# Turned tiles through SyncE's queue, weight transfers queued apart from their split, and consumers one unit later, in a two-layer encoder trunk

## The chip, the cores and the metric

The kernel runs on one core of one Trainium2 chip. The metric is device microseconds of one execution, the median of the runs; less is better. The profile is one further execution, taken by the hardware profiler.

## The reference, cut to what matters

Input is `x` of 256 rows by 2048, in float32. Layer 1 is forgetting attention with an MLP, layer 2 is chunked attention against a shared K/V with another MLP:

```python
u = rms_norm(h, a_norm_g)
q, k, v, fz = jnp.split(u @ a_w_in, [D, 2 * D, 3 * D], axis=-1)      # D = 2048, 16 heads of 128
q = rms_norm(q per head, a_q_g);  k = rms_norm(k per head, a_k_g)
s = q @ k.T * scale + c[query] - c[key]      # c: running sum of log sigmoid(fz + b_f), causal
h = h + (softmax(s) @ v) @ a_w_out
h = h + relu(rms_norm(h) @ w1)**2 @ w2       # w1: 2048 x 8192, w2: 8192 x 2048
k_sh, v_sh = jnp.split(rms_norm(h) @ kv_w, [D], axis=-1);  k_sh = rms_norm(k_sh per head)
q = rms_norm(rms_norm(h) @ b_w_q per head)
s = q @ k_sh.T * scale + rel_bias            # causal in chunks of 64
h = h + (softmax(s) @ v_sh) @ b_w_out
h = h + relu(rms_norm(h) @ w1)**2 @ w2       # second layer's weights
```

All products with weights are of float32 accuracy. The weights come to about 400 MB and each is read once.

## The kernel before, in words

**Units and panels.** Weights are cut into 768 units of 128 partitions by 1024 float32 (512 KB). A unit is loaded into a `raw` tile by SyncE's queue (SP, line 114; four `raw` buffers), and split on the chip into `hi` (ScalarE, line 116, rounded to float32r) and `lo` (VectorE, line 117, the rest), three buffers each. A panel is 8 units: 256 rows by 512 columns of output, accumulated in PSUM. For each unit the function `products` (lines 294 to 296) makes 12 matmuls of 128x512: hi·hi, hi·lo and lo·hi for two k-tiles and two row blocks. `fetch` keeps the splits of two units ahead of the one that is multiplied (`AHEAD = 2`); `issue` queues a unit's transfer and its split together. 8 units make a panel, and the units run in this order: layer 1's q, k and v panels for each of four head groups (units 0 to 95), its output projection (96 to 127), its MLP in four chunks of w1 and w2 (128 to 383), layer 2's q (384 to 415), the shared k and v by head group (416 to 479), output projection (480 to 511), MLP (512 to 767). Where a stage is `woven`, its first two panels alternate unit by unit.

**Turning a tile.** What comes out of a panel has its rows on partitions; the next product needs columns there. `blocks32` (line 168) transposes 32x32 blocks on VectorE into a tile `z`. `carry` moves the blocks through DRAM: `rows` (line 178) writes `z` to the DRAM tile `turn` in one DMA, `columns` (line 184) reads it back in four DMAs of 32 partitions. Both are issued by GpSimd (POOL), `nc.gpsimd.dma_start`. There are 92 such round trips: 60 of 512 KB (hidden activations, q, k and residual panels) and 32 of 192 KB (one for each head's softmax, through `flip`).

**The list of fills.** `run_fill` runs once behind each unit's products and takes the next entry of the deque `fill`; `add_fill` lays a list of entries over it. `carry` returns `[[rows], [], [columns]]`: rows behind the first unit after the panel, columns behind the third. The consumers lie further back: the hidden activations' `take` (lines 513 to 519), the residual panels' `use` (`split_turned`, lines 160 to 162) and `scale_q` (line 337) behind the sixth unit; in `attend`, the four heads' `softmax` (lines 352 to 369) behind units 6 to 9 of the v panel and what follows, and `values` (lines 382 to 386) behind units 13 to 16.

**What sets the order.** Each engine executes its own list of instructions in order, and waits on semaphores. These lists are not the order in which the Python code names the operations: the framework places each engine's instructions by a plan of its own when the program is built, with the code's order as a priority. So the place of a fill in the code is a wish, and the profile shows the place that was given.

Of the kernel before, what the change touches and what calls it, by code (L numbers as in the profile page):

```python
# [10 lines left out]
F32R = mybir.dt.float32r  # L11
# [4 lines left out]
P = 128  # L16
# [10 lines left out]
NEG = -1.0e30  # L27
UN = 1024
AHEAD = 2
UA = UN // 512  # L30
REL = 384

# [2 lines left out]
def trunk(ctx: ExitStack, tc: tile.TileContext, xT, xr, gs, hg, bf, wgate, w_in, w_oa, w1a, w2a,  # L35
          w_kv, w_qb, w_ob, w1b, w2b, rel, out):
    nc = tc.nc
    V, S, G, TE = nc.vector, nc.scalar, nc.gpsimd, nc.tensor

    def pool(name, bufs, **kw):  # L40
        return ctx.enter_context(tc.tile_pool(name=name, bufs=bufs, **kw))

    PSUM = bass.MemoryType.PSUM
    wsp = pool("wsp", 3)
# [35 lines left out]
    units = deque()  # L80

    def queue(src, first, woven):
        u = [src[i] for i in range(first, first + KT // UA * NG)]
        n = KT // UA
        if woven:
            u[: 2 * n] = [u[i + q * n] for i in range(n) for q in range(2)]
        units.extend(u)
# [15 lines left out]
    queue_mlp(w1b, w2b)  # L103
    ready = deque()

    def issue(parts=1):
        src = units.popleft()
        raw = wraw.tile([P, UN], F32, name="raw")
        hi = wsp.tile([P, UN], F32R, name="hi")
        lo = wsp.tile([P, UN], F32R, name="lo")  # L110
        n = UN // parts
        cuts = [slice(i * n, (i + 1) * n) for i in range(parts)]
        for c in cuts:
            nc.sync.dma_start(raw[:, c], src[:, c])
        for c in cuts:
            S.activation(hi[:, c], raw[:, c], AF.Copy)  # L116
            V.tensor_tensor(lo[:, c], raw[:, c], hi[:, c].bitcast(F32), op=ALU.subtract)  # L117
        ready.append((hi, lo))

    def fetch(ahead=AHEAD):  # L120
        while units and len(ready) <= ahead:
            issue()
        return ready.popleft()

    fill = deque()

    def run_fill():
        if fill:
            for f in fill.popleft():
                f()  # L130
# [5 lines left out]
    def acc_pair():  # L136
        t = ps_acc.tile([P, 2 * 512], F32, name="acc")
        return [t[:, i * 512 : (i + 1) * 512] for i in range(2)]
# [32 lines left out]
    def carry(z, dst):  # L171
        w = z.shape[1]
        n = w // 4
        box = []

        def rows():
            box.append(dram.tile([P, w], F32, name="turn", tag=f"turn{w}", bufs=4))
            G.dma_start(box[0], z)  # L178

        def columns():  # L180
            s = box[0].rearrange("(i a) f -> a i f", i=4)
            d = dst.rearrange("p (i f) -> p i f", i=4)
            for j in range(4):
                G.dma_start(d[32 * j : 32 * j + 32], s[:, :, j * n : (j + 1) * n])  # L184

        return [[rows], [], [columns]]

    def turned(name="q", **kw):
        z = qkv.tile([P, GH * T], F32, name="z")
        return z, qkv.tile([P, GH * T], F32, name=name, tag=name, **kw)  # L190

    def next_x(n, r2, stats, which, into, kept=None):
        add_h = residual(n, r2)
        zt = []

        def use(flipped=False, which=which, into=into):
            t = zt[1].rearrange("p (i k b c) -> p k b i c", i=4, k=GH, b=NB)
            if flipped:
                t = t[:, :, :, ::-1, ::-1]
            split_turned(t, n, which, into)  # L200

        def f(b, ps):
            add_h(b, ps)
            stats.add(b, n)
            if b == 0:
                zt.extend(turned(bufs=4))
            blocks32(h[b][:, n * 512 : (n + 1) * 512], zt[0], b)
            if b == NB - 1:
                add_fill(carry(*zt) + [[], [], [use]])
                if kept is not None:  # L210
                    kept.append(use)
        return f
# [75 lines left out]
    def products(ps, hi, lo, x, u):  # L288
        for j in range(UA):
            k = u * UA + j  # L290
            wh, wl = hi[:, j * 512 : (j + 1) * 512], lo[:, j * 512 : (j + 1) * 512]
# [6 lines left out]
    def panels(x, evacs, before=None):  # L298
        ps = [acc_pair() for _ in evacs]
        for u in range(KT // UA):  # L300
            if before:
                before(u)
            for q, evac in enumerate(evacs):
                hi, lo = fetch(min(u, AHEAD) if before else AHEAD)
                products(ps[q], hi, lo, x, u)
                run_fill()
                if u == KT // UA - 1:
                    for b in range(NB):
                        evac(b, ps[q][b])
# [25 lines left out]
    def scale_q(land, layer):  # L335
        q = qkv.tile([P, GH, T], F32, name="q", bufs=4)
        S.activation(q.rearrange("p a (b i c) -> p (a b) i c", b=NB, i=4),
                     land.rearrange("p (i ab c) -> p ab i c", i=4, c=32), AF.Copy, scale=gqk[:, layer : layer + 1])
        return q

    def residual(n, r2=None):
        def f(b, ps):
            hc = h[b][:, n * 512 : (n + 1) * 512]
            if r2 is None:
                V.tensor_tensor(hc, ps, hc, op=ALU.add)
            else:
                V.scalar_tensor_tensor(hc, ps, r2[:, b : b + 1], hc, op0=ALU.mult, op1=ALU.add)
        return f
# [39 lines left out]
    def attend(g, q, k, v, bias, cq, o):  # L388
        st = [{} for _ in range(GH)]
        k4 = k.rearrange("p (i a b c) -> p a b i c", i=4, a=GH, b=NB)  # L390
        A = [[lambda a=a: softmax(st[a], g, a, q(), k4, bias(), cq() if cq else None)] for a in range(GH)]
        C = [[lambda a=a: values(st[a], a, v, o, g * GH + a)] for a in range(GH)]
        return [[]] * 5 + A + [[]] * 3 + C

    def v_evac(v, r):
        def f(b, ps):
# [3 lines left out]
    def add_fill(items):  # L400
        for i, it in enumerate(items):
            if i < len(fill):
                fill[i] = fill[i] + it
            else:
                fill.append(it)
# [85 lines left out]
    for g in range(NG):  # L491
        zq, lq = turned("z")
        box = {}
        panels(x, [lambda b, ps: head_norm(st0.e, zq, lq)(b, ps)], load_x if g == 0 else None)
        add_fill([[]] * 5 + [[lambda box=box, lq=lq: box.update(q=scale_q(lq, 0))]])
        if g == 0:
            add_fill([[], [], [], [st0.spread]] + gates(x, st0))
        if g == 1:
            for b in range(NB):
                nc.sync.dma_start(h[b], xr[b])  # L500
        zk, k = turned("k")
        v = qkv.tile([P, NB, 512], F32, name="v")
        panels(x, [head_norm(st0.e, zk, k)])
        add_fill([[]] * (4 if g == 0 else 0) + [[lambda g=g, box=box: box.update(b=decay_bias(g))]])
        add_fill([[]] * (3 if g == 0 else 0) + attend(g, lambda box=box: box["q"], k, v, lambda box=box: box["b"], lambda: ct["cq"], o))
        panels(x, [v_evac(v, st0.r)])

    def mlp(x, st, last):
        for c in range(NCH):
            hid = []  # L510

            def take(t):
                S.activation(t, t, AF.Relu)  # L513
                y = acts.tile([P, 2, GH, T], F32R, name="act")
                hi, lo = (y[:, i].rearrange("p k (b i c) -> p (k b) i c", b=NB, i=4) for i in range(2))
                t = t.rearrange("p (i kb c) -> p kb i c", i=4, c=32)
                S.activation(hi, t, AF.Square)  # L517
                S.activation(t, t, AF.Square)  # L518
                V.tensor_tensor(lo, t, hi.bitcast(F32), op=ALU.subtract)  # L519
                hid.extend(y[:, :, j, :] for j in range(GH))  # L520

            def turn_hidden():
                zt = []

                def f(b, ps):
                    if b == 0:
                        zt.extend(turned(bufs=4))
                    blocks32(ps, zt[0], b)
                    if b == NB - 1:
                        add_fill(carry(*zt) + [[], [], [lambda: take(zt[1])]])  # L530
                return f

            stage(x, [turn_hidden() for _ in range(NG)], c == 0)
            stage(hid, [(last if c == NCH - 1 else residual)(n, st.r2) for n in range(NG)], True)
# [10 lines left out]
    qs, evs = [], []  # L545
    for g in range(NG):
        box = {}

        def f(b, ps, box=box):
            if b == 0:  # L550
                z, lq = turned("z")
                box["f"] = head_norm(st2.e, z, lq)
                add_fill([[]] * 5 + [[lambda: qs.append(scale_q(lq, 1))]])
            box["f"](b, ps)
        evs.append(f)
    stage(xb, evs, True)
# [11 lines left out]
    for g in range(NG):  # L568
# [3 lines left out]
        box = {}  # L572
# [70 lines left out]
```

## Time and profile before

| | us |
|---|---|
| three runs, median (lowest to highest) | 2296.51 (2289.01 to 2299.11) |
| the profiled execution's own time | 2314.15 |
| its span, first to last instruction | 2312.4 |
| TensorE busy (matmuls) | 2205.8 |
| VectorE busy | 1264.0 |
| ScalarE busy | 1048.6 |
| GpSimd busy | 305.1 |
| SP's DMA queue, share of 16 engines over the span | 56.2% |
| GpSimd's DMA queue, share of 16 engines | 11.2% |
| granted TensorE clock, mean | 0.978 |

In the profile a line such as `PE s L352 <- DMA k<-turn: 40.4, 8, 7.0` says who waited, at which line of the kernel, for what, for how many microseconds in total, how often, and how long at most. In a timeline a row has the start, the duration, the engine, the line, the operation, the tiles written and read, and in brackets the engine's idle time before it with what ended it. `x4` marks four such instructions merged into one row. Engine PE is TensorE, DVE is VectorE, ACT is ScalarE, POOL is GpSimd, SPq is the queue of DMAs that SyncE issues.

### The profile page before, as it was taken

How to read it: one execution, taken by the hardware profiler on the slowest of the kernel's cores; microseconds unless marked ns; L12 is line 12 of the kernel's file. 1: busy time of each engine (PE TensorE's matmuls, PEld its weight loads, DVE VectorE, ACT ScalarE, POOL GpSimd, SP SyncE). 2: the span in 40 equal slices, each digit the busy share in tenths (PEclk: the TensorE clock that was granted, in tenths of full speed). 3: DMA queues.
4: the chain of work that ended last, by engine and by line, in shares of the span. 5: the costliest groups of instructions: out<-in, count | busy, mean ns of one | idle time of the engine just before them, and what ended most of it. 6: DMA issues, size and time to landing. Idle time of an engine off the chain costs nothing. (4 is left out here: it accounts for less than half of the span.)

```text
span 2312.4 us, 26023 instructions
## 1 busy us (share of the span) xinstructions
PE 2205.8 (95%) x9518; PEld 1798.3 (78%) x9518; DVE 1264.0 (55%) x1478; ACT 1048.6 (45%) x1251; POOL 305.1 (13%) x508
## 2 busy tenths in 40 slices
PE   7998899999999999999998798999999999999999
PEld 4777777888877877888877677788878788878877
DVE  4666555655544554554655465566554555545554
ACT  4444444654344345344563344446443443443443
POOL 0232222110000001001102122221100100100000
PEclk8999999999999999999999999999999999999999
DMA  6666666877666666667766566668766676765675
GB/s 204 218 213 205 194 215 209 257 236 226 192 218 209 193 216 217 195 219 234 234 212 216 184 200 200 191 211 248 236 206 194 229 223 193 229 215 191 219 232 169
DMA packets 144241, 491.64 MB, mean 213 GB/s; under 512 B 20576, under 2 KB 24816, under 8 KB 143856
## 3 DMA queue, kind: packets, MB, share of 16 engines
q1 hardware_dynamic: 117808, 414.44, 56.2%
q0 software_dynamic: 26304, 75.53, 11.2%
q8 instruction: 75, 1.23, 0.2%
q14 instruction: 54, 0.44, 0.1%
HBM read 450.01 MB, written 39.87 MB: 212 GB/s over the span
## 5 line engine op out<-in xcount | busy, mean ns | idle before, releaser
L117 DVE TENSOR_TENSOR lo<-raw,hi 128x1024 fp32r<-128x1024 f32 (+1 forms) x770 | 932.8, 1217 | 841.4 <-ACT hi L116 840.9
L294 PE MATMUL acc<-hi,act 128*128 128x512 f32 x3072 | 1215.6, 396 | 38.4 <-ACT hi L116 19.3
L116 ACT ACTIVATE hi<-raw 128x1024 fp32r<-128x1024 f32 (+1 forms) x770 | 809.3, 1056 | 956.2 <-PE acc L296 903.2
L295 PE MATMUL acc<-lo,act 128*128 128x512 f32 x3072 | 1215.5, 396 | 17.7 <-DVE lo L117 16.9
L296 PE MATMUL acc<-hi,act 128*128 128x512 f32 x3072 | 1206.7, 393 | 1.5 <-DVE act L152 1.4
L294 PEld LDWEIGHTS acc<-hi,act 128*128 128x128 f32 x3072 | 583.2, 190 | 171.1 <-ACT hi L116 26.1
L295 PEld LDWEIGHTS acc<-lo,act 128*128 128x128 f32 x3072 | 583.7, 190 | 157.0 <-DVE lo L117 37.7
L296 PEld LDWEIGHTS acc<-hi,act 128*128 128x128 f32 x3072 | 583.5, 190 | 124.0 <-DVE act L152 3.5
L178 POOL DMA_DIRECT2D turn<-z x92 | 52.4, 570 | 1358.7 <-DVE z L168 1320.6
L184 POOL DMA_DIRECT2D q<-turn x176 | 96.0, 552 | 197.9 <-issue 117.6
L513 ACT ACTIVATE q<-q 128x1024 f32<-128x1024 f32 x32 | 33.9, 1058 | 110.0 <-DMA q<-turn 110.0
L184 POOL DMA_DIRECT2D prT<-turn x128 | 69.9, 552 | 35.0 <-DMA turn<-z 23.9
L326 POOL TENSOR_TENSOR rn<-vv,mhalf 128x4 f32<-128x4 f32 x32 | 46.1, 1440 | 192.7 <-DVE vv L324 192.5
L366 ACT ACTIVATE pr<-t,nm 128x128 f32<-128x128 f32 x64 | 28.5, 446 | 65.3 <-DVE nm L365 65.2
L352 PE MATMUL s<-k,q 128*128 128x128 f32 x64 | 17.6, 369 | 40.4 <-DMA k<-turn 40.4
L352 PEld LDWEIGHTS s<-k,q 128*128 128x128 f32 x64 | 16.1, 265 | 46.7 <-issue 33.4
L519 DVE TENSOR_TENSOR act<-q,act 128x1024 fp32r<-128x1024 f32 x32 | 39.2, 1224 | 21.2 <-ACT q L518 21.2
L168 DVE STREAM_TRANSPOSE z<-acc 128x512 f32<-128x512 f32 x64 | 41.9, 693 | 5.2 <-PE acc L296 5.2
L322 DVE TENSOR_REDUCE ss<-sq 128x4 f32<-128x512 f32 x32 | 21.7, 677 | 38.6 <-ACT sq L320 38.6
L328 DVE TENSOR_TENSOR qn<-acc,rn 128x512 f32<-128x512 f32 x32 | 22.1, 691 | 31.4 <-POOL rn L326 31.4
L320 ACT ACTIVATE sq<-acc 128x512 f32<-128x512 f32 x32 | 18.9, 595 | 39.5 <-DVE qn L328 21.8
L518 ACT ACTIVATE q<-q 128x1024 f32<-128x1024 f32 x32 | 33.8, 1056 | 0.8
(104 smaller groups left out, 564.3 us busy)
## 6 DMA issues: line engine op xcount, KB each, us to landing
raw<-in_w1a SPq DMA_DIRECT2D x128, 512.0 KB, 4.3
raw<-in_w2a SPq DMA_DIRECT2D x128, 512.0 KB, 4.3
raw<-in_w1b SPq DMA_DIRECT2D x128, 512.0 KB, 4.4
raw<-in_w2b SPq DMA_DIRECT2D x128, 512.0 KB, 4.3
raw<-in_w_in SPq DMA_DIRECT2D x94, 512.0 KB, 5.0
raw<-in_w_kv SPq DMA_DIRECT2D x64, 512.0 KB, 4.9
turn<-z POOLq DMA_DIRECT2D x60, 512.0 KB, 5.1
q<-turn POOLq DMA_DIRECT2D x176, 128.0 KB, 5.6
```

The source lines that it names most:

```text
L116: S.activation(hi[:, c], raw[:, c], AF.Copy)
L117: V.tensor_tensor(lo[:, c], raw[:, c], hi[:, c].bitcast(F32), op=ALU.subtract)
L168: V.transpose(z.rearrange("p (j n b c) -> p b n j c", j=4, n=n, b=nb)[:, b], src.rearrange("p (n j c) -> p n j c", n=n, j=4))
L178: G.dma_start(box[0], z)
L184: G.dma_start(d[32 * j : 32 * j + 32], s[:, :, j * n : (j + 1) * n])
L294: TE.matmul(ps[b], xh, wh, start=k == 0, stop=False)
L295: TE.matmul(ps[b], xh, wl, start=False, stop=False)
L296: TE.matmul(ps[b], xl, wh, start=False, stop=k == KT - 1)
L326: G.tensor_tensor(rn, vv, mhalf, op=ALU.pow)
L513: S.activation(t, t, AF.Relu)
L518: S.activation(t, t, AF.Square)
L519: V.tensor_tensor(lo, t, hi.bitcast(F32), op=ALU.subtract)
```

## The change

Three edits go together.

1. `rows` and `columns` are issued by `nc.sync` in place of `nc.gpsimd`: 92 writes and 368 reads of `turn` join the 770 weight transfers on SP's queue, and GpSimd issues no DMA any more.
2. `issue` is cut in two. `load` takes a `raw` tile and queues the transfer; `issue` takes the oldest loaded unit and splits it. `fetch` splits as far ahead as before, and then loads until `EARLY = 3` loaded units stand beyond the last one split. The number of `raw` buffers stays four. In the first panel the two distances grow with the unit's number.
3. `carry` returns six entries in place of three, the last three empty, and consumers are laid one entry later: `use`, `take` and `scale_q` behind the seventh unit, `softmax` behind units 7 to 10, `values` behind units 14 to 17.

```diff
+EARLY = 3
...
-    def issue(parts=1):
+    raws = deque()
+
+    def load(parts=1):
         src = units.popleft()
         raw = wraw.tile([P, UN], F32, name="raw")
-        hi = wsp.tile([P, UN], F32R, name="hi")
-        lo = wsp.tile([P, UN], F32R, name="lo")
         n = UN // parts
         cuts = [slice(i * n, (i + 1) * n) for i in range(parts)]
         for c in cuts:
             nc.sync.dma_start(raw[:, c], src[:, c])
+        raws.append((raw, cuts))
+
+    def issue(parts=1):
+        if not raws:
+            load(parts)
+        raw, cuts = raws.popleft()
+        hi = wsp.tile([P, UN], F32R, name="hi")
+        lo = wsp.tile([P, UN], F32R, name="lo")
         for c in cuts:
             S.activation(hi[:, c], raw[:, c], AF.Copy)
             V.tensor_tensor(lo[:, c], raw[:, c], hi[:, c].bitcast(F32), op=ALU.subtract)
         ready.append((hi, lo))
 
-    def fetch(ahead=AHEAD):
-        while units and len(ready) <= ahead:
+    def fetch(ahead=AHEAD, early=EARLY):
+        while (units or raws) and len(ready) <= ahead:
             issue()
+        while units and len(raws) < early:
+            load()
         return ready.popleft()
...
         def rows():
             box.append(dram.tile([P, w], F32, name="turn", tag=f"turn{w}", bufs=4))
-            G.dma_start(box[0], z)
+            nc.sync.dma_start(box[0], z)
...
             for j in range(4):
-                G.dma_start(d[32 * j : 32 * j + 32], s[:, :, j * n : (j + 1) * n])
+                nc.sync.dma_start(d[32 * j : 32 * j + 32], s[:, :, j * n : (j + 1) * n])
 
-        return [[rows], [], [columns]]
+        return [[rows], [], [columns], [], [], []]
...
-                add_fill(carry(*zt) + [[], [], [use]])
+                add_fill(carry(*zt) + [[use]])
...
-                hi, lo = fetch(min(u, AHEAD) if before else AHEAD)
+                hi, lo = fetch(min(u, AHEAD), min(u // 2, EARLY)) if before else fetch()
...
-        return [[]] * 5 + A + [[]] * 3 + C
+        return [[]] * 6 + A + [[]] * 3 + C
...
-        add_fill([[]] * 5 + [[lambda box=box, lq=lq: box.update(q=scale_q(lq, 0))]])
+        add_fill([[]] * 6 + [[lambda box=box, lq=lq: box.update(q=scale_q(lq, 0))]])
...
-                        add_fill(carry(*zt) + [[], [], [lambda: take(zt[1])]])
+                        add_fill(carry(*zt) + [[lambda: take(zt[1])]])
...
-                add_fill([[]] * 5 + [[lambda: qs.append(scale_q(lq, 1))]])
+                add_fill([[]] * 6 + [[lambda: qs.append(scale_q(lq, 1))]])
```

## The prediction

> **What bounds the kernel now.** First the page's busy shares, then TensorE's waits, then the timelines around the longest of them.
>
> ```profile
> PE 2205.8 (95%) x9518; PEld 1798.3 (78%) x9518; DVE 1264.0 (55%) x1478; ACT 1048.6 (45%) x1251; POOL 305.1 (13%) x508
> PE s L352 <- DMA k<-turn: 40.4, 8, 7.0
> PE acc L294 <- ACT hi L116: 19.3, 15, 2.6
> PE acc L295 <- DVE lo L117: 16.9, 35, 0.9
> ACT q L513 <- DMA q<-turn: 110.0, 28, 7.2
> ACT q L337 <- DMA z<-turn: 30.4, 6, 7.1
> SPq L114 <- DVE lo L117: 1768.0, 712, 14.6
> ```
>
> TensorE bounds it: 9216 weight matmuls at 0.227 us from start to start (the timeline's spacing between stalls) are 2092 us of a 2312.4 us span; only the rest, some 220 us, can move. Of that, about 30 us are the first panels' start and 45 us the attention's own matmuls. What waits on a round trip is the first line in full, and much of the next two, because ScalarE, standing at L513 or L337 for a landing, splits the next unit late. SP always waits for a `lo` to free a `raw` buffer, so a transfer's start is set by the buffer, not by where the code queues it.
>
> One k round trip, layer 2, second head group (GpSimd's and TensorE's timelines), and the DMA packets between the write's issue and the columns' issue, with each queue's share of 16 engines:
>
> ```profile
> 1368.87 0.61 POOL L178 DMA_DIRECT2D turn<-z  x1 [2.78 <-DVE z L168]
> 1375.77 2.19 POOL L184 DMA_DIRECT2D k<-turn  x4 [6.29 <-DMA turn<-z]
> 1383.44 0.64 PE L352 MATMUL s<-k,q 128*128 128x128 f32 x2 [4.61 <-DMA k<-turn]
> 1386.44 0.63 PE L295 MATMUL acc<-lo,act 128*128 128x512 f32 x1
> 1386.87 0.47 PE L296 MATMUL acc<-hi,act 128*128 128x512 f32 x1
> 1387.41 0.40 PE L295 MATMUL acc<-lo,act 128*128 128x512 f32 x1
> 1387.64 0.40 PE L296 MATMUL acc<-hi,act 128*128 128x512 f32 x1
> ```
>
> ```profile
> q1 hardware_dynamic: 424, 1.56, 66.9%
> q0 software_dynamic: 144, 0.52, 18.8%
> raw<-in_w_kv SPq DMA_DIRECT2D x3, 512.0 KB, 5.8
> turn<-z POOLq DMA_DIRECT2D x1, 512.0 KB, 6.6
> ```
>
> The trip takes 14.6 us (1368.87 to 1383.44). The write needs 18.8% of 7.0 us, 1.3 us of all engines, yet lands after 6.6, among packets of three weight transfers, two of which were issued after it. And a stall costs more than its length: behind it matmuls start 0.43 us apart, later 0.23. In the stretches 162 to 360 and 1295 to 1503 us the granted clock is 0.94 and 0.93, a loss of 0.06 x 198 + 0.07 x 208 = 26 us for some ten stalls: 2.6 us each.
>
> The order that is executed is not the code's:
>
> ```profile
> 15.79 0.65 SPq L500 DMA_DIRECT2D h<-in_xr  x1
> 16.49 0.43 SPq L416 DMA_DIRECT2D xin<-in_xT  x1
> ...
> 1806.80 1.06 ACT L116 ACTIVATE hi<-raw 128x1024 fp32r<-128x1024 f32 x1 [1.66 <-PE acc L296]
> 1812.53 1.06 ACT L513 ACTIVATE q<-q 128x1024 f32<-128x1024 f32 x1 [4.67 <-DMA q<-turn]
> 1813.50 1.04 ACT L116 ACTIVATE hi<-raw 128x1024 fp32r<-128x1024 f32 x1
> 1815.85 0.50 PE L295 MATMUL acc<-lo,act 128*128 128x512 f32 x1 [0.68 <-DVE lo L117]
> ```
>
> Line 500 stands in the code of group 1 and is issued among group 0's first inputs. Counting L116 ahead of L513, nearly every `take` stands after 7 splits of the next panel, though the code names it after 8. Counting matmuls ahead of L352, the first softmax of a group stands at 7.5 to 7.8 units into the v panel, though the code allows 6. The builder placed them where it reckoned the data landed; the third and fourth softmax stand where the code names them.
>
> **The change, part by part.** *Early loads.* A transfer still waits for its `lo` four units back, so it starts no sooner; only its rank against other DMAs on SP changes. No term. In the first panel it may put a load before or after an `xin`: 0, bounds -4 to +4 us (waits there are 0.5 to 3.2 us each).
>
> *One unit later.* Where the builder had already placed a consumer later than its old place, the new place binds only if it is later still. `take` stands earlier than its place: nothing. The first softmax can't stand before 7.0 now. By itself this edit is worth about nothing, and it does not move the eight k stalls.
>
> *SP's queue.* The trip on SP is not in the trace. Nearest row: weight transfers of the same 512 KB on SP, 4.4 us from issue to landing (median), behind at most one other. Then the write is 4.4, the four columns three issues of 0.39 (`xin`, 128 KB) and 4.4 more, with 0.3 for the hand-over 10.3: 4.3 us saved of 14.6. The other end is issue time alone: (0.57 - 0.33) + 4 x (0.55 - 0.39) = 0.9 us. If each hop stands behind one more weight transfer (66.9% of 7.0 us over three: 1.6 us each), it is 3.2 worse: -2.3. I take 3.0, near the row of the same size and queue, less something for standing in line.
>
> The Trainium skill, "DMA: Bandwidth & Descriptors", Issuing engines are not separate DMA queues, says that transfers from any engine share the same 16 DMA engines, so another issuer saves only issue time. By it the saving is the 0.9. The 6.6 us for 1.3 us of packets speaks for more, since on one queue later transfers should stand behind; the case is a rival below.
>
> A faster trip may also be reckoned faster by the builder, which then places consumers earlier. For k the floor is 7.0 units, 0.5 to 0.8 units of 2.72 us, so 1.4 to 2.3 us earlier; I take 1.2 on average over both cases.
>
> - k: wait 5.05 each falls by 3.0 - 1.2 = 1.8, x 8 = 14; the clock's 2.6 x 8 falls by the same third, 7. Together -21.
> - MLPs: TensorE's waits there on `hi`, `lo` and `z` sum to 18.7 us (10.8 in the first, 7.9 in the second), about 0.6 us a `take`. Saving 3.0 ends them if the place holds; if it moves a split earlier (2.72) nearly nothing is won. Half: -9, and 2 for the clock. -11.
> - `scale_q`: waits on `hi` and `lo` in 162 to 360 and 1168 to 1304 us sum to 15.3. Half: -7, and 2 for the clock. -9. The 6.5 us on L328 there is PSUM's evacuation and stays.
> - GpSimd loses 460 issues, 0.26 ms of its 0.31; its `pow` (L326) waits for VectorE, not for them (192.5 us on L324). 0.
> - SP now waits at `rows` for z and at `columns` for the landing, with weight transfers queued behind, and every split behind those. z and `lo` come from VectorE in order, so `rows` costs little; `columns` can hold up to a write's landing, 4.4 to 5.1 us. Cover: pairing the n-th transfer with the n-th L116, it lands 4.2 us (median) before it is needed, and splits run two units ahead, 5.4 us less 2.3 us for `hi` and `lo`, 3.1. So in the MLPs 0. Around the attention 22 loads had under 1 us. There I take 10, bounds 0 to 48 (first rival).
>
> Sum: -21 - 11 - 9 + 10 = -31. The profiled execution took 2314.15 us (span 2312.4, 1.8 around it), 17.6 above the median of the runs; it would take 2283, and the median 2296.5 - 31 = 2265.
>
> **The rivals.** *Loads starve at the softmax trips* (slower). Four heads' columns each hold SP for a 192 KB write's landing, 3.6 us (median), in some 20 us. If two fall on one load, 7.2 - (0.3 + 3.1) = 3.8 us of stall and 2.2 of clock a group, eight groups: +48; it decides once a load is held over 3.4 us. With k's 21 gained and the rest lost, 2296.5 + 48 - 21 = 2323. For: SP has never waited on a landing so far, and loads are late just there. Against: the builder can put loads ahead of the columns.
>
> *The builder moves consumers a split earlier*, with the trip 3.0 faster: MLP and `scale_q` gain nothing, 2296.5 - 21 + 10 = 2285, on the edge of same and faster.
>
> *Only issue time is saved, places held*: k 8 x 0.9 x 1.5 = 11, MLP 10, `scale_q` 5, SP 10: 2281. *Only issue time, places earlier*: each of 28 takes 1.8 us later against its place, 50, SP 10: 2357. The rule of the skill cited above gives these two.
>
> **How the numbers follow.** Forecast 0.38, own range 2240 to 2282. Starving loads 0.25; moved consumers 0.15; issue time with held places 0.12, with earlier ones 0.10. About 0.5% (11.5 us) is what a measurement of this kernel can tell from none. Faster: 0.38, half of the moved and most of the held case, 0.52; same 0.13; slower 0.25 and 0.10, 0.35. At the low end the full 4.3 us on every trip and no SP cost: k -40, MLP -20, `scale_q` -13: 2224. At the top the starving case with some spread, 2338; beyond it lies most of the 2357 case.
>
> **What would show it.** Right: `turn<-z` on SP lands in 4 to 5 us, waits of L352 fall from 40 to about 26, L513's from 110 to under 80, PE's clock above 0.978. Wrong: SP's own waits name `turn` with tens of us and TensorE's waits on `hi` for `raw` grow around L352 (starving); L513 stands after 6 splits (builder); `turn<-z` still takes over 5 us.

## The result, and the profile after

| | before | after |
|---|---|---|
| median of six runs each, us (lowest to highest) | 2296.24 (2288.53 to 2299.64) | 2305.56 (2303.8 to 2307.73) |
| the profiled execution, us | 2314.15 | 2303.8 |
| granted TensorE clock, mean | 0.978 | 0.978 |

The changed kernel is slower by 0.5%: ratio 1.0048, with a 95% interval of 1.0027 to 1.0068, a small loss but clear of the noise. The two profiled executions would say the opposite, because before's lies 17.9 us above its own median and after's does not; so profiles of changed kernels are compared here with each other, and times by the ratio of the runs.

The page of the changed kernel: busy shares, and DMA issues with KB each and the median us from issue to landing.

```profile
PE 2199.6 (96%) x9518; PEld 1802.2 (78%) x9518; DVE 1267.9 (55%) x1478; ACT 1050.0 (46%) x1251; POOL 47.6 (2%) x48
...
turn<-z SPq DMA_DIRECT2D x60, 512.0 KB, 4.1
q<-turn SPq DMA_DIRECT2D x176, 128.0 KB, 5.5
```

Its waits:

```profile
ACT act L396 <- PE po L394: 117.5, 28, 9.3
...
PE acc L306 <- DVE lo L126: 44.1, 29, 3.6
...
PE acc L305 <- ACT hi L125: 29.4, 20, 2.7
...
ACT hi L125 <- DMA raw<-in_w_in: 14.1, 10, 2.9
...
ACT q L524 <- DMA q<-turn: 0.6, 1, 0.6
```

Everything that the change was reckoned to shorten is gone altogether: k's 40.4 us on TensorE have no line any more, `take`'s 110 us on ScalarE are 0.6 (it stands behind eight splits of the next panel now, not seven). The first line of the listing stood in the kernel before as

```profile
ACT act L385 <- PE po L383: 10.1, 10, 2.5
```

It has grown from 10.1 to 117.5 us: ScalarE stands at the copy of `values` (L396) until TensorE reaches that head's product `po`. TensorE's own waits for splits (`hi`, `lo`) have doubled, from 36.2 to 73.5 us. No DMA is among what TensorE waits for in this trace, and ScalarE waits for landings for 32.4 us in all.

Layer 1, third head group's k panel, where `values` of the second group are due; ScalarE's timeline, then TensorE's waits and `po` in it:

```profile
223.90 0.60 ACT L331 ACTIVATE sq<-acc 128x512 f32<-128x512 f32 x1 [2.89 <-DVE qn L339]
224.39 0.38 ACT L396 ACTIVATE act<-po 128x256 fp32r<-128x256 f32 x1
224.65 1.06 ACT L125 ACTIVATE hi<-raw 128x1024 fp32r<-128x1024 f32 x1
235.01 0.38 ACT L396 ACTIVATE act<-po 128x256 fp32r<-128x256 f32 x1 [9.30 <-PE po L394]
235.29 2.94 ACT L125 ACTIVATE hi<-raw 128x1024 fp32r<-128x1024 f32 x3
```

```profile
225.76 0.49 PE L305 MATMUL acc<-hi,act 128*128 128x512 f32 x1 [1.80 <-ACT hi L125]
229.46 0.80 PE L306 MATMUL acc<-lo,act 128*128 128x512 f32 x1 [3.21 <-DVE lo L126]
...
234.59 0.39 PE L394 MATMUL po<-prT,v 128*128 128x128 f32 x2
236.39 0.49 PE L305 MATMUL acc<-hi,act 128*128 128x512 f32 x1 [1.42 <-ACT hi L125]
237.65 0.80 PE L306 MATMUL acc<-lo,act 128*128 128x512 f32 x1 [0.77 <-DVE lo L126]
```

TensorE has used up every split when it comes to the head's `po`, and the next split stands behind the copy that waits for this `po`. Three splits are then made at once (2.94 us, from 235.29 on): their weights had landed at 219.87, 221.42 and 223.94. Count, in ScalarE's own order, the splits ahead of a `values` copy, and in TensorE's the units ahead of its `po`: the difference is the lead. Before, the four heads of a group have between 2.2 and 3.0 splits of lead; after, there are 2.0 for the first, 0.4 to 1.0 for the second, and 0.1 or none for the third and fourth, in all eight groups.

SP's queue, one stretch earlier, shows what lies among what. The second listing is the same stretch of the run without early loads (below):

```profile
206.26 0.34 SPq L189 DMA_DIRECT2D turn<-z  x1
206.64 0.43 SPq L115 DMA_DIRECT2D raw<-in_w_in  x1
207.20 1.79 SPq L195 DMA_DIRECT2D prT<-turn  x4
209.64 0.34 SPq L189 DMA_DIRECT2D turn<-z  x1
210.08 1.62 SPq L115 DMA_DIRECT2D raw<-in_w_in  x1
211.80 1.80 SPq L195 DMA_DIRECT2D prT<-turn  x4
```

```profile
196.41 0.34 SPq L187 DMA_DIRECT2D turn<-z  x1
196.86 1.99 SPq L193 DMA_DIRECT2D prT<-turn  x4
202.03 0.34 SPq L187 DMA_DIRECT2D turn<-z  x1
202.48 3.71 SPq L193 DMA_DIRECT2D prT<-turn  x8
206.29 1.80 SPq L115 DMA_DIRECT2D raw<-in_w_in  x4
```

With early loads each of the softmax's trips is parted from the next by a weight transfer; without them all trips come first and four transfers follow in one go.

### The profile page after: what moved, and what is told of

Read it like the earlier page. It is cut to its first block, busy times and chain, and to the rows that moved or that the text cites. A ratio compares the mean times of both kernels' runs of the same rounds, so it can differ in the third digit from the quotient of the medians.

```text
span 2301.7 us, 25837 instructions
## 1 busy us (share of the span) xinstructions
PE 2199.6 (96%) x9518; PEld 1802.2 (78%) x9518; DVE 1267.9 (55%) x1478; ACT 1050.0 (46%) x1251; POOL 47.6 (2%) x48
## 5 line engine op out<-in xcount | busy, mean ns | idle before, releaser
L126 DVE TENSOR_TENSOR lo<-raw,hi 128x1024 fp32r<-128x1024 f32 (+1 forms) x770 | 935.5, 1218 | 793.8 <-ACT hi L125 785.8
L305 PEld LDWEIGHTS acc<-hi,act 128*128 128x128 f32 x3072 | 585.4, 191 | 177.8 <-ACT hi L125 34.9
L396 ACT ACTIVATE act<-po 128x256 fp32r<-128x256 f32 x32 | 12.3, 384 | 117.5 <-PE po L394 117.5
L397 DVE TENSOR_TENSOR act<-po,act 128x256 fp32r<-128x256 f32 x32 | 13.5, 422 | 87.2 <-ACT act L396 87.2
L377 ACT ACTIVATE pr<-t,nm 128x128 f32<-128x128 f32 x64 | 28.7, 449 | 26.3 <-DVE nm L376 25.7
L339 DVE TENSOR_TENSOR qn<-acc,rn 128x512 f32<-128x512 f32 x32 | 22.1, 691 | 32.4 <-POOL rn L337 32.4
L528 ACT ACTIVATE act<-q 128x1024 fp32r<-128x1024 f32 x32 | 34.0, 1062 | 1.0
L171 ACT ACTIVATE z<-q,gsb 128x256 f32<-128x256 f32 x64 | 27.4, 495 | 3.2 <-DMA q<-turn 2.2
L358 DVE SCALAR_TENSOR_TENSOR h<-acc,qn,h 128x512 f32<-128x512 f32 x32 | 22.6, 747 | 11.0 <-PE acc L307 11.0
```

What stands on the lines that cost most here:

```text
L305: TE.matmul(ps[b], xh, wh, start=k == 0, stop=False)
L377: S.activation(pr[:, c], t[:, c], AF.Exp, bias=nm[:, b : b + 1], accum_out=su[:, b : b + 1])
```

## The experiments

Each ratio is to runs of the kernel before on the same chip. The three edits are SP's queue, early loads and later consumers.

| run | what it has | median us | ratio to before (95%) |
|---|---|---|---|
| after | SP's queue, early, later | 2305.56 | 1.0048 (1.0027 to 1.0068) |
| e12 | early | 2296.24 | 1.0001 (0.9972 to 1.0029) |
| e4 | later | 2277.12 | 0.9910 (0.9878 to 0.9941) |
| e5 | SP's queue | 2231.83 | 0.9717 (0.9690 to 0.9744) |
| e3 | SP's queue, later | 2213.38 | 0.9627 (0.9605 to 0.9648) |
| e8 | SP's queue, early | 2313.32 | 1.0054 (1.0032 to 1.0077) |
| e1 | after, softmax's trips on GpSimd | 2219.54 | 0.9653 (0.9633 to 0.9673) |
| e2 | after, only softmax's trips on SP | 2328.67 | 1.0129 (1.0087 to 1.0172) |
| e6 | after, softmax's columns on GpSimd | 2218.47 | 0.9652 (0.9627 to 0.9677) |
| e7 | after, softmax's rows on GpSimd | 2290.14 | 0.9965 (0.9948 to 0.9982) |
| e9 | after, `values` behind the newest split | 2266.13 | 0.9882 (0.9863 to 0.9901) |
| e13 | e9, head norm behind it too | 2254.18 | 0.9798 (0.9770 to 0.9825) |
| e14 | e13, second block's norm two splits later | 2231.62 | 0.9711 (0.9666 to 0.9756) |
| e10 | e3, `values` behind the newest split | 2220.69 | 0.9687 (0.9666 to 0.9707) |
| e11 | e6 without early loads | 2193.03 | 0.9564 (0.9543 to 0.9586) |

**Which trips, which edit (e1 to e4).** The softmax's trips are told by their width. In `carry` of the changed kernel:

```diff
+        dge = nc.sync if z.shape[1] == GH * T else nc.gpsimd
-            nc.sync.dma_start(box[0], z)
+            dge.dma_start(box[0], z)
-                nc.sync.dma_start(d[32 * j : 32 * j + 32], s[:, :, j * n : (j + 1) * n])
+                dge.dma_start(d[32 * j : 32 * j + 32], s[:, :, j * n : (j + 1) * n])
```

> The changed kernel, but the 32 softmax round trips of 192 KB go back to GpSimd's queue; the 60 trips of 512 KB stay on SP. Theory A (order): in the changed kernel the softmax trips' columns on SP make the builder put the weight transfers later in its plan, so ScalarE's copy of each `values` result stands in its list before splits that TensorE needs to get there; TensorE then runs out of split weights. Without them the splits stand three units ahead again and the attention stretches lose about 90 us of stalls: 2215 us, between 2200 and 2240, and the MLPs stay without stalls. Theory B (the later consumers are the loss, values stand one unit later here too): no better than the changed kernel, 2295 to 2310. Theory C (weights arrive late on the chip because SP is held by the trips): half to all of the gain, 2215 to 2260, with weights landing earlier before their split than in the changed kernel.

2219.54 us, ratio 0.9653: with these 32 of the 92 trips off SP's queue, the 86 us between it and the changed kernel are back, and ScalarE's wait at the copies falls from 117.5 to 3.6 us. The second run turns the line round (`dge = nc.gpsimd if z.shape[1] == GH * T else nc.sync`):

> The changed kernel, but the 60 trips of 512 KB go back to GpSimd's queue; only the 32 softmax trips stay on SP. Theory A: the attention's loss stays in full, and the gain of the changed kernel in k's wait and in the MLPs is given back: 2340 us, between 2320 and 2370, with L396 on ScalarE again waiting for TensorE by over 60 us and TensorE waiting for k's landing by about 40 us. Theory B: the loss comes from the later consumers, so the same as with both on GpSimd plus nothing: 2300 to 2320. Theory C: fewer bytes on SP than in the changed kernel, so less starving: 2290 to 2310.

2328.67 us, the slowest of all: it has the loss (ScalarE's wait for `po`, 100.4 us) and little of the gain (`take` waits 92.1 us, k 26.3). The third takes the early loads out of the changed kernel's `fetch`:

```diff
-        while units and len(raws) < early:
-            load()
```

> The changed kernel without the early loads: a transfer is queued with its split, as before. If early loads only give the weights a rank ahead of the trips (the prediction: worth nothing), 2300 to 2310. Theory A: with a lower rank the weights stand still later in the plan around the softmax trips, and the hidden activations' consumers are placed a split earlier: 2330 us, between 2315 and 2360. Theory C: weights late on the chip, 2330 to 2360 as well, but seen as ScalarE's splits waiting for landings by tens of us.

2213.38 us, 92 below the changed kernel. The expectation fell: it is the early loads that harm most, not the softmax's trips by themselves (e11, below, prices these trips' columns without early loads). Its waits:

```profile
ACT act L394 <- PE po L392: 61.0, 24, 5.0
...
PE acc L304 <- DVE lo L126: 7.5, 12, 0.8
...
PE acc L303 <- ACT hi L125: 5.0, 9, 1.6
```

ScalarE still waits at the copies, but TensorE hardly does: the lead here is 1.0, 0, 0 and up to 1, yet three heads' `po` stand together at one unit, so a group seems to have one short stop instead of three or four: a lead of nought would be paid per stop, not per copy. The fourth run is the kernel before with the consumers one unit later, nothing else (`use` and `take` as in the change, not shown here):

```diff
-        return [[rows], [], [columns]]
+        return [[rows], [], [columns], [], [], []]
-        return [[]] * 5 + A + [[]] * 3 + C
+        return [[]] * 6 + A + [[]] * 3 + C
...
-        add_fill([[]] * 5 + [[lambda box=box, lq=lq: box.update(q=scale_q(lq, 0))]])
+        add_fill([[]] * 6 + [[lambda box=box, lq=lq: box.update(q=scale_q(lq, 0))]])
```

> The kernel before with consumers one unit later and nothing else: all trips on GpSimd, loads queued with their split. Theory A and the prediction's step: no effect that counts, 2290 to 2305, k's waits as before or up to 1.4 us longer each because three of the eight first softmax matmuls stand at 7.0 instead of 7.5 units. Theory B: this edit carries the loss: 2330 us or more.

2277.12 us, ratio 0.9910: some 20 us gained, though k's waits only fall from 40.4 to 31.1 us and `take`'s from 110.0 to 77.5. Measured like the table of the next section, and against e12, which runs the very lists of the kernel before (shown below), the gain lies in the attentions (129.1 to 104.4 us) and most of it in layer 2's k and v panels, where the granted clock rises from 0.935 to 0.992. What in them it comes from stays open.

**The other parts, and rows against columns (e5 to e8).** SP's queue alone, in the kernel before:

```diff
-            G.dma_start(box[0], z)
+            nc.sync.dma_start(box[0], z)
-                G.dma_start(d[32 * j : 32 * j + 32], s[:, :, j * n : (j + 1) * n])
+                nc.sync.dma_start(d[32 * j : 32 * j + 32], s[:, :, j * n : (j + 1) * n])
```

> All round trips on SP's queue, weight transfers and consumers as before. Theory (the loss needs the early loads and the softmax's columns on SP's queue together): no early loads, so no loss; faster than before, but some 20 us short of the run without early loads (2213), which has the later consumers: about 2235. Rival (the softmax's trips on SP lose by themselves, the later consumers pay for it): not faster than before, 2300 or more.

2231.83 us, as the theory had it. In the changed kernel only the softmax's columns go back to GpSimd (`dge` of e1 in the loop of `columns`, `nc.sync` in `rows`):

> The changed kernel, with the softmax's column transfers alone put back on GpSimd's queue; its writes (rows) stay on SP, early loads and later consumers too. Theory: ScalarE's values copies stand three splits ahead of TensorE again, 2215 to 2225, as with the whole trip on GpSimd (2220). Rival (the writes on SP hold the early loads): near the changed kernel, 2290 to 2310.

2218.47 us, and ScalarE's wait for `po` is 1.0 us. The mirror, `dge` in `rows` alone:

> The mirror of the run before it: the softmax's writes alone put back on GpSimd's queue, its columns on SP among the early loads. Theory: ScalarE's values copies lose their lead as in the changed kernel, 2290 to 2320. Rival (the writes hold the queue): 2215 to 2230.

2290.14 us, with 103.5 us at the copies: it is the four column DMAs of a softmax, among early loads on SP's queue. Last, the changed kernel with the consumers at their old places:

```diff
-                add_fill(carry(*zt) + [[use]])
+                add_fill(carry(*zt)[:5] + [[use]])
-        return [[]] * 6 + A + [[]] * 3 + C
+        return [[]] * 5 + A + [[]] * 3 + C
...
-        add_fill([[]] * 6 + [[lambda box=box, lq=lq: box.update(q=scale_q(lq, 0))]])
+        add_fill([[]] * 5 + [[lambda box=box, lq=lq: box.update(q=scale_q(lq, 0))]])
```

> The changed kernel with the consumers at their old places: SP's queue and the early loads together. Theory: the order is as bad as in the changed kernel, which has the later consumers to mend what they can: 2300 to 2330. Rival (the later consumers are what sets ScalarE's copies late): faster than the changed kernel, 2260 or less.

2313.32 us, ratio 1.0054: no better than the changed kernel, so the later consumers do not set ScalarE's copies late.

**Is it the order, or the transfers? (e9 to e14).** The rows so far cannot part two readings: SP's queue gives the builder a bad order for ScalarE, or it makes weights or columns late on the chip. That TensorE waits for no landing in the changed kernel speaks for the first. So do SP's own waits for a softmax's or a tile's write to land before it issues the columns, first in the changed kernel, then in e3:

```profile
SPq L195 <- DMA turn<-z: 110.7, 58, 4.0
...
SPq L193 <- DMA turn<-z: 122.9, 60, 4.1
```

e5 has 123.3 us of them and e11, the fastest of all, 119.0: SP is held as long in the fast kernels as in the slow one. e9 then leaves SP's list exactly as it is in the changed kernel (GpSimd's too, TensorE's but for two of 9518 places in the traces) and ties the copies to the newest split:

```diff
+            last[0] = S.activation(hi[:, c], raw[:, c], AF.Copy)
+            last[1] = V.tensor_tensor(lo[:, c], raw[:, c], hi[:, c].bitcast(F32), op=ALU.subtract)
...
+        with tc.issue_after(last[0].ins):
+            S.activation(o[i][:, 0], po[:, :T], AF.Copy)
+        with tc.issue_after(last[1].ins):
+            V.tensor_tensor(o[i][:, 1], po[:, :T], o[i][:, 0].bitcast(F32), op=ALU.subtract)
```

> The changed kernel, SP's queue with its early loads and trips in the same order; only ScalarE's copy of values stands behind the newest split that the code has issued, and VectorE's second half behind that split's lo, so each stands one split later. Theory (the loss is those copies, which stop the splits while they wait for TensorE): the lead is 1 to 2 splits instead of 0 to 1, most of the attention's stalls go, 2225 to 2255. Rival (the loads or the columns land late on the chip because they share SP's queue): 2290 or more.

2266.13 us, between the two: 39 us of the 92, less than expected. The third group's k panel again, ScalarE's timeline of this run:

```profile
210.40 0.60 ACT L332 ACTIVATE sq<-acc 128x512 f32<-128x512 f32 x1 [2.14 <-PE acc L308]
213.89 0.60 ACT L332 ACTIVATE sq<-acc 128x512 f32<-128x512 f32 x1 [2.89 <-DVE qn L340]
214.39 1.05 ACT L126 ACTIVATE hi<-raw 128x1024 fp32r<-128x1024 f32 x1
```

Here the split stands behind the head norm's second square, which waits 2.89 us for VectorE and GpSimd. Counted in splits, the two squares at the end of the third group's q panel (56 units) stand after 57 and 57 in the changed kernel and in e9, but after 58 and 60 in the kernel before, in e3 and in e11. So the copies are not alone in standing too early; the norm behind a panel does too. e13 ties the norm too:

```diff
+            with tc.issue_after(last[0].ins):
+                S.activation(sq, ps, AF.Square)
...
+            with tc.issue_after(last[1].ins):
+                V.tensor_reduce(ss, sq.rearrange("p (a d) -> p a d", a=GH), axis=AX.X, op=ALU.add)
```

> The run with the splits ahead of values, and the head norm's square (ScalarE) and sum (VectorE) of q and k also behind the newest split; SP's queue with its early loads and trips nearly as changed. Theory (the rest of the loss is the same fault at the head norm: its squares stand after 57 splits at the end of the q panel, after 58 and 60 where the attention runs well): another 15 to 30 us off 2266, 2236 to 2251. Rival (what is left is SP's queue itself, loads or columns landing late): 2260 or more.

2254.18 us: 12 more, short of the range; both squares then stand after 58, and the second still waits 2.90 us ahead of a split. e14 puts the second block's square and sum two more splits later, at 58 and 60:

```diff
+        for e in list(late):
+            e[0] -= 1
+            if e[0] == 0:
+                tc.add_manual_dep(e[1], last[0].ins.name, NOSYNC, reason="order")
+                tc.add_manual_dep(e[2], last[1].ins.name, NOSYNC, reason="order")
+                late.remove(e)
...
+            if b == 1:
+                late.append([2, i0.ins, i1.ins])
```

> The run before it, with the second block's square and sum of each head norm two more splits later, so that the squares stand after 58 and 60 splits at the end of the first such q panel, as before the change; still early loads and all trips on SP's queue. Theory (order of ScalarE's and VectorE's lists is the whole loss): most of the 40 us that are left, 2215 to 2235; by the later z a k softmax stands up to 2 units later, which may hold some of it. Rival (a rest that belongs to SP's queue on the chip): 2245 or more.

2231.62 us. In ratios, the step from e3 to the changed kernel is 0.0421, and e14 takes back 0.0337 of it: four fifths of the loss comes back by edits to the order in which ScalarE and VectorE do their work, with early loads and all trips still on SP's queue. But e14 is not a clean edit: against the changed kernel SP's list differs in 109 of 1269 places and TensorE's in 244 of 9518, and some k softmax stands up to 2.3 units later. With SP's list untouched it is e9's share that is shown, 0.0166 of 0.0421 or two fifths; e13, where 11 places of SP's list differ, takes back 0.0250, three fifths.

The same tie in the run without early loads:

> The run without early loads, with the same forced order of values behind the newest split. Theory: it lost little to the copies (67 us above the ideal in both attentions, against 59 with the softmax's trips on GpSimd), so 5 to 15 us less than 2213: 2198 to 2210. Rival (the copies' place is worth nothing where they are stacked): 2213.

2220.69 us, 7 slower by the medians and 0.6% by the ratios: the expectation fell. The lead there rises to 2 or 3, but ScalarE then waits for weights, which in this kernel go out in one burst behind the trips (`ACT hi L126 <- DMA raw<-in_w_in` 34.2 us, longest 10.3; 12.9 us in e3). Which list is good depends on what SP's queue does.

**The best of the parts.** e6 without the early loads:

> The softmax's columns on GpSimd's queue and no early loads, the rest as changed. Theory: the attention of the run with the columns on GpSimd and the MLPs of the run without early loads, 2218 less some 11 us: 2203 to 2212. Rival (early loads help once the columns are away): 2220 or more.

2193.03 us, ratio 0.9564, better than expected and faster than both kernels. Its waits, and ScalarE where the other kernels stall:

```profile
PE acc L304 <- ACT act L160: 11.7, 6, 2.5
...
PE acc L304 <- DVE qn L338: 6.5, 1, 6.5
...
PE acc L304 <- ACT hi L125: 1.3, 2, 1.1
...
ACT act L395 <- PE po L393: 1.1, 3, 0.5
```

```profile
204.28 0.60 ACT L330 ACTIVATE sq<-acc 128x512 f32<-128x512 f32 x1 [2.07 <-PE acc L306]
204.78 1.05 ACT L125 ACTIVATE hi<-raw 128x1024 fp32r<-128x1024 f32 x1
206.19 0.38 ACT L395 ACTIVATE act<-po 128x256 fp32r<-128x256 f32 x1 [0.37 <-PE po L393]
208.94 1.06 ACT L125 ACTIVATE hi<-raw 128x1024 fp32r<-128x1024 f32 x1 [2.37 <-PE acc L306]
209.91 0.58 ACT L330 ACTIVATE sq<-acc 128x512 f32<-128x512 f32 x1
```

A split stands between the two squares and ahead of the copies; no wait of ScalarE at a copy is over 0.5 us. Three kernels differ from it by one edit or two. With the softmax's columns on SP's queue (e3) it is slower by 0.63% in the ratios, 14 us (20 by the medians); with early loads (e6) by 0.88%, 20 us (25), 11 of them in the MLPs; with both (the changed kernel) by 4.84%, 111 us. So each costs something without the other, and the two together cost far more than their sum. And the early loads alone, in the kernel before:

> Weight transfers three units ahead as the only edit; round trips on GpSimd's queue and consumers as before. Theory (early loads harm only among the trips on SP's queue) and the prediction's no term: as before, within 0.5%. Rival (their rank harms ScalarE's order by itself): slower by 1% or more.

2296.24 against 2296.18 us: nothing. The traces say why: in every engine's list, SP's 809 DMAs and TensorE's 9518 matmuls included, each instruction of e12 stands at the same place as in the kernel before. There the edit changes nothing that runs, so e12 can't tell what early loads would do to GpSimd's trips on the chip. It also makes the two profiles two executions of the same lists, and they differ: 2314.15 and 2299.89 us, with 110.0 and 89.0 us of `take`'s waits and 40.4 and 41.9 of k's.

## Why the prediction was wrong

To size its terms, take from each trace the time above 0.2267 us a matmul, by stage (us; the attentions' column has the output projection behind each, where the last group's `values` fall, and their own matmuls, 45 us by the prediction):

| | first group | both attentions | layer 2's q | MLPs |
|---|---|---|---|---|
| before | 34.9 | 127.8 | 12.8 | 36.8 |
| before's lists once more (e12) | 37.2 | 129.1 | 11.2 | 20.6 |
| SP's queue alone (e5) | 37.1 | 82.9 | 10.6 | 0.8 |
| SP's queue, later (e3) | 38.1 | 67.0 | 9.4 | 0.8 |
| after | 36.9 | 142.5 | 12.1 | 10.2 |
| after, reordered (e14) | 36.9 | 73.5 | 9.2 | 10.4 |
| best (e11) | 35.5 | 46.6 | 9.3 | 0.8 |

The first two rows have the same lists, so some 16 us of the MLPs' 36.8 belong to that one execution.

- **"Early loads. No term" is the step that failed.** Its argument, that a transfer waits for its `lo` anyway, holds as far as the runs show: SP still waits 1416.7 us for `lo`, and alone the edit changes nothing (e12). But beside SP's trips it takes the ratio from 0.9627 to 1.0048, 92 to 97 us, and with the old consumers from 0.9717 to 1.0054, some 77. From e3 to the changed kernel, 230 of 1269 places in SP's list and 337 of 1251 in ScalarE's have another instruction. The prediction itself said that the edit changes the rank of transfers on SP, and that each engine's list is placed when the kernel is built; it did not join the two.
- **SP holding the loads, +10 (bounds 0 to 48): right place, wrong mechanism.** The first rival named the softmax's trips and TensorE's waits on splits, and its 2323 came nearer than the forecast, which is luck: weights were not starved. ScalarE waited 14.1 us for `raw<-in_w_in` and 117.5 us for `po`, and SP's holds, 110.7 us in the changed kernel and 119.0 in e11, leave e11's attentions at 46.6 us. (That SP had never waited on a landing is not quite so: before, it did for some 6 us in all.) The price was some 75 us in the attentions (142.5 against 67.0), above the bound, as it was drawn from how long a load is held and not from what else is placed ahead of a split.
- **SP's queue: mechanism right, sizes too small.** The gain forecast without SP's cost was 41 us; e5 gained 65 (0.0283 of 2296). By the table, with e12's row for the kernel before, the MLPs were given 11 and lost some 20 of 20.6 us, as `take`'s wait ends whole, and the attentions lost 46. Two terms were mis-sized. From the write's issue to the last column's landing the trip of a `q` tile (hidden and residual panels) takes 13.5 us in the kernel before and 9.0 in e5 (medians of 44): 4.5 saved where 3.0 was taken, just over the upper end of 4.3. And consumers were not placed earlier to eat 1.2 of it: in e5 the first softmax of a group came up to a unit later, and nearly every `take` still stands after 7 splits. The rule of the Trainium skill that the prediction weighed ("DMA: Bandwidth & Descriptors", Issuing engines are not separate DMA queues) would have it at issue time, 0.9 us; the measurement does not agree.
- **One unit later, "worth about nothing": wrong.** It gains 20 us alone, and again 0.9% on SP's queue without early loads (0.9717 to 0.9627). With early loads nearly all of that is lost (1.0054 and 1.0048).
- **GpSimd relieved, 0:** right as far as shown. In e11 GpSimd issues 128 column DMAs again, and is faster than e3.
- **What would show it** misled. Three of the four signs of being right came true (`turn<-z` lands in 4.1 us, and the waits of L352 and L513 are all but gone); only the clock, 0.978 as before, did not. Of the signs of being wrong, SP's waits on `turn` came to 110.7 us and TensorE's on `hi` grew, but the first does not suffice for the second, as e3 and e11 have the first without the second. `ACT act <- PE po`, a wait of an engine with half its time idle, was the line to look for.

The chain of causes is shown as far as this: early loads together with the softmax's columns on SP's queue carry most of the loss (e3, e6 and e11 beside the changed kernel), the lists that they give have copies and norms ahead of splits (counted), and moving the copies alone gives back two fifths with SP's list untouched (e9). That the order of the other engines is four fifths rests on e14, whose SP list also moved. Open stays the last fifth, some 19 us; the MLPs' 10 us are half of that, and all kernels with both early loads and `take`'s trips on SP's queue have them, but no run sets them apart. That the builder ranks the splits late because it reckons their weights behind the columns is what the lists suggest; its reckoning itself was not seen.

## What to carry to other kernels

Where a builder lays out the lists, prefetching early on a queue that also carries work with a consumer can change in which order every engine's list is laid out, and not only when transfers start: after such an edit, count in each engine's own list what stands ahead of the operations that feed the bound engine. Where an idle engine waits long for the bound engine and that one waits for the idle engine's next item, suspect the order; one forced order tests it without touching the queue. Where an edit seems to be worth nothing, compare the lists first: it may have changed none of them. Try each part of a combined edit alone and in pairs: here SP's queue gained 2.8% and later consumers 0.9%, early loads alone changed no list, and the three together lost 0.5%.

## What the runs showed of the hardware

- The same round trip takes longer or shorter by its queue and what shares it. The `q` tiles' trip takes 13.5 us on GpSimd's queue in the kernel before (12.6 in e4, 13.3 in e2, which has early loads) and 9.0 on SP's in e5 (8.9 in e3); with early loads beside it on SP's queue it takes 11.7 (the changed kernel). Each 128 KB column lands 5.6 us after its issue on GpSimd's queue. On SP's queue alone (e5) it is 3.3, in the listing below; with the changed kernel's early loads it is 5.5, in the listing of the result.

```profile
turn<-z SPq DMA_DIRECT2D x60, 512.0 KB, 3.7
q<-turn SPq DMA_DIRECT2D x176, 128.0 KB, 3.3
```

- The granted clock goes with the stalls, not with the queue: it is 0.978 before and after, 0.988 in e5, and 0.992 in e3 and e11. Over the panels of the two attentions it is 0.940 and 0.935 before, and 1.000 in e11, where they hardly stall.
- One profiled execution can mislead about a stage: two executions of the same lists had 36.8 and 20.6 us above the matmuls' pace in the MLPs.
